# Reordering the prompt attention of a hybrid decoder step: transposes, fills, roots and the last heads

## The chip, the cores and the metric

The kernel runs on one core of one Trainium2 chip. The metric is the device time of one execution in microseconds (us); lower is better. Engines are named as the profile names them: PE is TensorE (matrix multiplies and transposes), ACT is ScalarE, DVE is VectorE, POOL is GpSimd, and SP is the queue that issues nearly all of the DMAs.

## What is computed

One layer of a decoder, for a prompt of 1024 tokens and for 8 samples of 4 new tokens each (32 rows, which the kernel treats as tile 8 behind the eight prompt tiles of 128 rows). Only the parts that the change touches are shown:

```python
u, v, cq, ckv, kpe = split_in(rms_norm(xp, g_mix[l]) @ w_in[l])
a_out, _ = chunk_gmlp(u, v, w_s[l], b_s[l], ln_v_g[l], ln_v_b[l])
ckv_n = rms_norm(ckv, g_kv_a[l])
q = mla_queries(cq, pos_p, g_q_a[l], w_uq[l], g_qk_q[l])      # 8 heads x 96, normalised and rotated
k, vv = mla_keys_values(ckv_n, kpe, pos_p, w_uk[l], w_uv[l], g_qk_k[l])
b_out = mla_prompt_attend(q, k, vv)                           # causal softmax over 1024 keys
xp = xp + merge_out(a_out, b_out, g_out_a[l], g_out_b[l], w_o[l])

def merge_out(a_out, b_out, g_out_a, g_out_b, w_o):
    return jnp.concatenate([rms_norm(a_out, g_out_a), rms_norm(b_out, g_out_b)], axis=-1) @ w_o
```

The same runs for the samples, whose attention reads 4096 cached tokens each; then follow a memory attention and a gated feed-forward block. All data are float32.

## The kernel before

**Matrix products.** `mm3` (line 179) makes a float32 product from three matmuls of a high and a low half (`h`, `l` at the end of names; `split`, line 187, cuts them: the high half on ScalarE, the low half on VectorE). Inside the prompt attention the low half of every split is put into a list, `self.lows`, and issued by the next `flush` (line 204).

**First stage** (`phase1`, line 288). The rows of x are projected to u, v and the latents. The root of each row's mean square stands in `rs_tok`, one column a tile of rows. `squares(c)` (line 342) squares three tiles on ScalarE and takes their root in about eleven small steps (`rsqrt_steps`, line 214) on VectorE, or for the later tiles on GpSimd. `squares(2)` does tiles 6, 7 and the 32-row tile 8 together. A planner orders this stage on all engines but SP.

**Prompt attention** (`phase2a`, line 646). From the line with `manual_schedule` on, PE, ACT, DVE and POOL run in the order in which the code emits the instructions; SP's order is left to the planner. A *unit* is one head and one half of the queries, (h, G) with G = 0 or 1, four query tiles each. `head_unit` (line 936) gives its parts: scores `a` (matmuls, and the evacuation with the row's maximum on VectorE), exponential `e` (ScalarE, line 969), transposes `T` of the probabilities (line 977, copied by ScalarE, line 979), products with the values `V` (line 992), `copy` and `out`. A unit with G = 0 takes three steps and one with G = 1 four, so the eight heads take 56 steps, counted by `t`. In each step the loop emits: the pending low halves, the transposes of the unit's probabilities, outputs that are due, the exponentials of the scores of the step before, the scores of the *next* unit (`jobs`), the low halves again, the value products of the step before, and then everything that is placed in `extra[t]`; last, one piece of each running generator in `steps`.

What is placed in `extra`, by hand: `preps[h]` (line 918), four pieces a head that transpose the keys and queries of one half, in the order k0, q0, k1, q1, and split them; the projections and norms of heads 4 to 7 (`late`, from `proj_group`, line 850, whose last pieces rotate the queries and finish the keys on GpSimd, lines 607 to 610 and 907); and the `weight_sums` (line 809), 26 pieces that load two weight blocks, make four sums on GpSimd (lines 822 to 825) and store them for the feed-forward block. They share two buffers, so each load waits for the store of two pieces before.

The generators are `sample_prep` (line 1014), started in step 31, which makes the samples' query operands and fills `cn`, `bd` and four blocks `bdq` on GpSimd; then `pages_ahead`; and at the end of the stage `mix` (through `mix_steps`, line 1575), which normalises, transposes and stores the attention's output rows for the merge.

**Sample attention** (`phase2b`, line 1118). Its loop over pairs of cached pages emits in the same manner; prompt tiles 4 to 7 go through `mix_steps` at fixed places of that loop.

Of the kernel before, what the change touches and what calls it, by code (L numbers as in the profile page):

```python
# [13 lines left out]
P = 128  # L14
# [140 lines left out]
class Net:  # L155
# [96 lines left out]
    def constants(self, pool):  # L252
        nc, I = self.nc, self.I
        self.cols = self.t(pool, [P, NCOL], F32, "cols")
        nc.sync.dma_start(self.cols, I["cols"])
        self.ident = self.t(pool, [P, P], F32, "ident")
        self.ones = self.t(pool, [P, P], F32, "ones")
        nc.gpsimd.memset(self.ones, 1.0)

        nc.scalar.activation(self.t(pool, [P, 1], F32, "gelu"), self.ones[:, :1], AF.Gelu_apprx_tanh)  # L260
        self.cn = self.t(pool, [P, 258], F32, "cn")
        self.kpe = self.t(pool, [P, 9, 32], F32, "kpe")
        self.rs_tok = self.t(pool, [P, 9], F32, "rs_tok")
        self.sq_tok = self.t(pool, [P, 9], F32, "sq_tok")
# [23 lines left out]
    def phase1(self):  # L288
# [53 lines left out]
        def squares(c):  # L342

            ss = self.t(pl, [P, 3], F32, "ss", 3)
            if c == 2:
                nc.vector.memset(ss, 1.0)
            for i in range(3):
                xt = xts[3 * c + i]
                nc.scalar.activation(xt, xt, AF.Square, accum_out=ss[: xt.shape[0], i : i + 1])
            for _ in self.rsqrt_steps(pl, self.rs_tok[:, 3 * c : 3 * c + 3], ss, 1.0 / 1024, nc.gpsimd if c else None):  # L350
                pass
# [18 lines left out]
        for c, (o, n) in enumerate(CH):  # L370
            for k in range(8):
                self.split(xh[:, k, o : o + n], xl[:, k, o : o + n], xrs[2 * c + k // 4][:, k % 4], self.col("g_mix", k))
            if c == 1:
                squares(0)
# [13 lines left out]
        squares(1)  # L388
# [42 lines left out]
        for hf in range(2):  # L431
# [8 lines left out]
            for i0, i1 in ((0, 3), (3, 6), (6, 8), (8, 9)):  # L440
                m, tn = i1 - i0, TILES[i0][1]
                if hf == 0 and i0 == 3:
                    squares(2)
# [202 lines left out]
    def phase2a(self):  # L646
# [28 lines left out]
        gs = [self.proj_group(p, pp, 0, *g, st[0], c, ("mm", 5)) for g in groups]  # L675
        (qk, v), (qk1, _), (qk2, _) = gs
        for f in qk + v + qk1[:9] + qk2[:3]:
            f()
        norm, norm_s = qk1[9:], qk2[3:]
# [10 lines left out]
        order = [(h, G) for h in range(6) for G in range(2)] + [(6, 0), (7, 0), (6, 1), (7, 1)]  # L690
        units = [self.head_unit(pm, pp, h, G, st[h // 4], c) for h, G in order]
        preps = [self.head_prep(pm, pp, h, st[h // 4], c) for h in range(8)]
        _, v1 = self.proj_group(p, pp, 0, *groups[1], st[0], c)
        late = [self.proj_group(p, pp, 1, *g, st[1], c) for g in groups]
# [40 lines left out]
        def mix(G, ring):  # L735
            n = self.t(p, [P, 4, 4, 96], F32, ring, 2).rearrange("p m h d -> p (m h d)")
            hl = n[:, 512:].rearrange("p (k n) -> p k n", k=4)
            yield from self.mix_steps(
                pm, pp, 1, 2 * G, 2 * G + 2, lambda i: b_all[:, i], lambda j: hl, lambda j: n[:, :512], ("tp", 4)
            )  # L740

        E = mybir.EngineType
        with tc.manual_schedule(engines={E.PE, E.Activation, E.DVE, E.Pool}):
# [17 lines left out]
            for n, u in enumerate(units):  # L761
                for k, banks in enumerate(u["steps"]):
# [32 lines left out]
            for f in V:  # L795
                f()
            for t in sorted(outs):
                for f in outs[t]:
                    f()
            while steps:  # L800
                steps = [x for x in steps if next(x, 0) is None]
        nc.sync.dma_start(self.b_dram, b_all[:, 4:])
# [211 lines left out]
    def sample_prep(self, pp):  # L1014
# [29 lines left out]
        nc.gpsimd.memset(self.cn, 0.0)  # L1044
# [73 lines left out]
    def phase2b(self):  # L1118
# [30 lines left out]
        for i, src in ((6, self.b_last), (4, b4)):  # L1149
            flat = place()  # L1150
            hl = flat[:, :1024].rearrange("p (k n) -> p k n", k=4)
            mix = self.mix_steps(
                pa, ppt, 1, i, i + 2, lambda e, src=src: src[:, e % 2], lambda j, hl=hl: hl,
                lambda j, flat=flat: flat[:, j * 512 : j * 512 + 512], ("m", 1),
            )
            for n in range(5):
                at(2 * n + (2 if i == 6 else 5), 0, lambda mix=mix: next(mix, 0))
# [417 lines left out]
    def mix_steps(self, p, pp, z, i0, i1, src, new, nt, tt):  # L1575
# [10 lines left out]
        yield  # L1586
# [4 lines left out]
        yield  # L1591
        for i, n in enumerate(ns):
# [9 lines left out]
            elif z:  # L1602
# [786 lines left out]
```

## Time and profile before

| | us |
|---|---|
| median of 3 runs | 1879.51 (1877.55 to 1879.68) |
| profiled execution | 1879.13 |
| its span, first to last instruction | 1877.4 |
| TensorE busy | 1820.9 (97%) |
| VectorE busy | 1351.9 (72%) |
| ScalarE busy | 927.3 (49%) |
| GpSimd busy | 700.4 (37%) |
| mean granted clock of TensorE | 0.987 of full speed |

The stages follow one another in time: the first stage to about 198 us, the prompt attention to about 434 us, the sample attention after it. A row of a timeline reads: start, length, engine, line of the kernel, operation, what is written and read, and in brackets the idle time of the engine before it with what ended that. Busy time on TensorE is modelled; at half clock the same matmul is busy for longer. The line numbers are those of the kernel before.

### The profile page before, as it was taken

The numbers are of one execution on the slowest core, as the hardware profiler recorded it, in microseconds if no ns is written. First come the engines' busy times: TensorE is split into PE (matmuls) and PEld (weight loads), VectorE is DVE, ScalarE is ACT, GpSimd is POOL, SyncE is SP. The second block draws the span as 40 slices with busy tenths as digits, with TensorE's granted clock in tenths as the row PEclk, the third lists the DMA queues.
The fourth block names the chain that finished last, engine by engine and source line by source line (L and its number), as shares of the span: only waits on it lengthen the run. The fifth ranks groups of instructions, "written<-read, shape, count | busy, mean of one in ns | idle before, by whom it ended". The sixth has DMA issues, their size and how long they took to land.

```text
span 1877.4 us, 39366 instructions
## 1 busy us (share of the span) xinstructions
PE 1820.9 (97%) x14222; PEld 1713.6 (91%) x14222; DVE 1351.9 (72%) x2800; ACT 927.3 (49%) x1965; POOL 700.4 (37%) x862
## 2 busy tenths in 40 slices
PE   9999899888999999999899999999999999999999
PEld 8899677668999999999799988999999999999999
DVE  7864756565877668776744676788888888878664
ACT  7335676565555565555533455633333333344442
POOL 2021246533444444453313110167776677500000
PEclk9999999899999999999999999999999999999999
DMA  8102054556776666664554345322223222495252
GB/s 314 46 17 71 23 184 142 163 173 174 227 207 181 184 183 186 176 181 121 187 166 135 130 151 155 128 72 76 85 75 97 69 70 79 109 354 165 79 153 75
DMA packets 153187, 261.18 MB, mean 139 GB/s; under 512 B 20897, under 2 KB 97538, under 8 KB 152994
## 3 DMA queue, kind: packets, MB, share of 16 engines
q1 hardware_dynamic: 152130, 257.63, 44.6%
q8 instruction: 112, 1.84, 0.4%
q10 hardware_dynamic: 864, 1.05, 0.2%
q14 instruction: 81, 0.66, 0.1%
HBM read 212.79 MB, written 45.82 MB: 138 GB/s over the span
## 4 chain that ended last, share of the span: by engine, by line
PE 78%; issue 6%; DVE 4%; DMA 4%; SPq 3%; POOL 2%; ACT 2%; POOLq 0%; DVEq 0%; ACTq 0%
PE s L185 13%; PE d L185 12%; PE mm L185 9%; PE b L185 8%; PE F L185 7%; PE X L185 7%; PE E L185 7%; PE A L185 3%; PE y L185 3%; PE o L992 2%; DMA cT<-cT 2%; PE tp L977 1%; SPq L1297 1%; SPq L1301 1%; PE tp L185 1%
## 5 line engine op out<-in xcount | busy, mean ns | idle before, releaser
L185 PE MATMUL s<-w2h,ch 128*128 128x288 f32 (+1 forms) x1024 | 305.1, 298 | 0.0
L185 PE MATMUL s<-w2h,cl 128*128 128x288 f32 (+1 forms) x1024 | 297.4, 290 | 4.2 <-POOL cl L1329 4.2
L185 PE MATMUL s<-w2l,ch 128*128 128x288 f32 (+1 forms) x1024 | 296.0, 289 | 0.0
L185 PEld LDWEIGHTS s<-w2h,ch 128*128 128x128 f32 x1024 | 194.0, 189 | 8.3 <-issue 2.5
L185 PEld LDWEIGHTS s<-w2h,cl 128*128 128x128 f32 x1024 | 193.8, 189 | 6.3 <-POOL cl L1329 6.3
L185 PEld LDWEIGHTS s<-w2l,ch 128*128 128x128 f32 x1024 | 194.3, 190 | 0.0
L1372 DVE TENSOR_REDUCE ss<-sq 128x16 f32<-128x1024 f32 x128 | 155.3, 1214 | 32.1 <-ACT sq L1369 31.6
L1329 POOL TENSOR_TENSOR cl<-cT,ch 128x512 fp32r<-128x512 f32 x64 | 82.8, 1294 | 124.9 <-ACT ch L1325 116.1
L1369 ACT ACTIVATE sq<-s 128x512 f32<-128x512 f32 x128 | 76.6, 598 | 89.7 <-PE s L185 89.7
L1366 ACT ACTIVATE sq<-s 128x512 f32<-128x512 f32 x128 | 76.8, 600 | 72.9 <-PE s L185 72.4
L191 ACT CAST a<-brb 128x528 fp32r<-128x528 f32 x77 | 48.8, 634 | 112.8 <-PE d L185 108.7
L185 PE MATMUL d<-a,w 128*128 128x264 f32 x768 | 95.4, 284 | 1.0 <-DVE G L2166 1.0
L185 PEld LDWEIGHTS d<-a,w 128*128 128x128 f32 x768 | 94.3, 188 | 1.2 <-issue 1.2
L192 DVE TENSOR_TENSOR a<-brb,a 128x528 fp32r<-128x528 f32 x77 | 54.4, 707 | 56.3 <-ACT a L191 56.3
L2037 POOL TENSOR_TENSOR lo<-s,hi 128x1024 fp32r<-128x1024 f32 x20 | 62.8, 3141 | 45.7 <-ACT hi L2036 45.7
L185 PE MATMUL mm<-whi,xh 128*128 128x256 f32 (+3 forms) x272 | 77.9, 288 | 0.0
L185 PE MATMUL mm<-wlo,xh 128*128 128x256 f32 (+3 forms) x272 | 77.5, 287 | 0.0
L185 PE MATMUL mm<-whi,xl 128*128 128x256 f32 (+3 forms) x272 | 77.4, 288 | 0.0
L2092 ACT COPY a<-A 128x264 f32<-128x264 f32 x43 | 16.1, 375 | 118.7 <-PE A L185 113.9
L1325 ACT CAST ch<-cT 128x512 fp32r<-128x512 f32 x128 | 73.4, 626 | 2.6 <-PE tp L1005 1.6
L185 PE MATMUL d<-a,hi 128*128 128x264 f32 x552 | 72.0, 284 | 0.0
L2155 POOL TENSOR_TENSOR cv<-cv,row 128x1056 f32<-128x1056 f32 x22 | 63.5, 2887 | 19.1 <-ACT cv L2154 19.1
(743 smaller groups left out, 6381.8 us busy)
## 6 DMA issues: line engine op xcount, KB each, us to landing
cT<-cT SPq DMA_DIRECT2D x256, 160.0 KB, 2.9
ck<-ck SPq DMA_DIRECT2D x256, 144.0 KB, 3.4
raw<-w_up SPq DMA_DIRECT2D x44, 512.0 KB, 3.6
wsumd<-wsum SPq DMA_DIRECT2D x26, 512.0 KB, 3.4
actd<-cv SPq DMA_DIRECT2D x44, 264.0 KB, 2.4
brb<-actd SPq DMA_DIRECT2D x44, 264.0 KB, 5.6
wsum<-w_down SPq DMA_DIRECT2D x22, 512.0 KB, 3.6
raw<-wsumd SPq DMA_DIRECT2D x20, 512.0 KB, 3.7
```

The lines of the kernel that those rows point to most:

```text
L185: self.nc.tensor.matmul(out, l, r, start=first and i == 0, stop=last and i == len(seq) - 1)
L191: {"act": nc.scalar.copy, "pool": nc.gpsimd.tensor_copy, "dve": nc.vector.tensor_copy}[eng](hi, src)
L192: low = lambda: nc.vector.tensor_tensor(lo, src, hi, ALU.subtract)
L977: nc.tensor.transpose(tp[:, z * P : z * P + P], u[e][:, j * P : j * P + P], self.ident)
L992: nc.tensor.matmul(u["o"][g : g + 64, o : o + m * P], s["v"][:, j, h % 4], th[:, z * P : (z + m) * P], start=j == 0, stop=b == len(banks) - 1,
L1325: nc.scalar.copy(d["h"][:, k], src[k])
L1329: (nc.vector if k else nc.gpsimd).tensor_tensor(d["l"][:, k], src[k], d["h"][:, k], ALU.subtract)
L1366: nc.scalar.activation(sq[:, 0], ps[:, :, n0 : n0 + 256], AF.Square)
L1369: nc.scalar.activation(sq[:, 1], pt.rearrange("p (e d) -> p e d", e=2), AF.Square)
L1372: yield lambda: nc.vector.tensor_reduce(s["ss"][:, g0 : g0 + 2].rearrange("p e (z h) -> p z e h", z=2), sq.rearrange("p z e (h d) -> p z e ...
L2037: eng.tensor_tensor(lo, src, hi, ALU.subtract)
L2155: nc.gpsimd.tensor_tensor(cv, cv, row, ALU.mult)
```

## The change

- *Roots.* `squares` takes a range of tiles and an engine. Tiles 6 and 7 are done together on GpSimd, tile 8 alone on VectorE. `rs_tok` is set to 1 once.
- *Sample tile's projection.* Queries and keys of heads 0 to 3 for tile 8 are projected within steps 0 to 6 and no longer ahead of the attention.
- *Transposes ahead.* The pieces of `preps` move so that scores follow their query tile by two steps or more (before, mostly one), and the first half's keys by three.
- *Last heads.* The order of units becomes (5,0), (6,0), (5,1), (7,0), (6,1), (7,1) where it was (5,0), (5,1), (6,0), (7,0), (6,1), (7,1).
- *Late projections and sums.* The second group of `late` moves one step ahead. 18 of the weight sums are placed in steps 4 to 28, none in 29 to 35, and 8 in steps 36 to 47; before, the 26 were spread evenly over steps 4 to 47.
- *Fills.* `sample_prep` emits the fills of `bdq` and `cn` first, and the copy into `qr` and the fill of `bd` one step later; all that follows comes one step later.
- *Merge.* `mix` runs over four tiles as one generator with finer pieces, in the prompt attention (tiles 0 to 3) and in the sample attention (tiles 4 to 7).

```diff
+        nc.vector.memset(self.rs_tok, 1.0)
...
-        def squares(c):
-            ss = self.t(pl, [P, 3], F32, "ss", 3)
-            if c == 2:
-                nc.vector.memset(ss, 1.0)
-            for i in range(3):
-                xt = xts[3 * c + i]
-                nc.scalar.activation(xt, xt, AF.Square, accum_out=ss[: xt.shape[0], i : i + 1])
-            for _ in self.rsqrt_steps(pl, self.rs_tok[:, 3 * c : 3 * c + 3], ss, 1.0 / 1024, nc.gpsimd if c else None):
+        def squares(i0, i1, e=None):
+            n, w = i1 - i0, TILES[i0][1]
+            ss = self.t(pl, [P, 3], F32, "ss", 4)[:w, :n]
+            for i in range(i0, i1):
+                nc.scalar.activation(xts[i], xts[i], AF.Square, accum_out=ss[:, i - i0 : i - i0 + 1])
+            for _ in self.rsqrt_steps(pl, self.rs_tok[:w, i0:i1], ss, 1.0 / 1024, e):
                 pass
...
-                    squares(2)
+                    squares(6, 8, nc.gpsimd)
+                    squares(8, 9)
...
-        gs = [self.proj_group(p, pp, 0, *g, st[0], c, ("mm", 5)) for g in groups]
-        (qk, v), (qk1, _), (qk2, _) = gs
-        for f in qk + v + qk1[:9] + qk2[:3]:
+        (qk, v), (qk1, _) = (self.proj_group(p, pp, 0, *g, st[0], c, ("mm", 5)) for g in groups[:2])
+        for f in qk + v + qk1[:9]:
             f()
-        norm, norm_s = qk1[9:], qk2[3:]
+        norm = qk1[9:]
...
-        order = [(h, G) for h in range(6) for G in range(2)] + [(6, 0), (7, 0), (6, 1), (7, 1)]
+        order = [(h, G) for h in range(5) for G in range(2)] + [(5, 0), (6, 0), (5, 1), (7, 0), (6, 1), (7, 1)]
...
+        tok_s, _ = self.proj_group(p, pp, 0, *groups[2], st[0], c)
...
-        spread(norm_s, 0, 4)
+        spread(tok_s, 0, 7)
         for h in range(1, 8):
             b = 7 * (h - 1)
-            put(preps[h], {3: (9, 10, 11, 13), 4: (22, 23, 25, 26), 6: (36, 37, 39, 40), 7: (40, 41, 44, 46)}.get(h, (b + 1, b + 2, b + 2, b + 4)))
+            put(preps[h], {3: (9, 10, 12, 13), 5: (28, 29, 34, 35), 6: (32, 33, 41, 42), 7: (39, 38, 44, 46)}.get(h, (b, b + 1, b + 3, b + 4)))
         spread(late[0][0], 11, 21)
-        spread(late[1][0], 15, 25)
+        spread(late[1][0], 14, 24)
         spread(late[0][1], 22, 27)
-        spread(late[1][1], 26, 31)
+        spread(late[1][1], 25, 30)
...
-            extra[4 + j * 45 // len(sums)].append(lambda x=x: self.weight_sums(half(), *x))
+            extra[4 + j * 26 // 18 if j < 18 else 36 + (j - 18) * 13 // 8].append(lambda x=x: self.weight_sums(half(), *x))
...
-        def mix(G, ring):
...
+        def mix():
+            n = [self.t(p, [P, 4, 4, 96], F32, r, 2).rearrange("p m h d -> p (m h d)") for r in "kq"]
+            hl = [x[:, 512:].rearrange("p (k n) -> p k n", k=4) for x in n]
+            for k, _ in enumerate(self.mix_steps(
+                pm, pp, 1, 0, 4, lambda i: b_all[:, i], lambda j: hl[j], lambda j: n[j // 2][:, :512], ("tp", 4)
+            )):
+                if k not in (0, 2):
+                    yield
...
-                            outs[t + 3].append(lambda: steps.extend((mix(0, "k"), mix(1, "q"))))
+                            outs[t + 3].append(lambda: steps.append(mix()))
...
-            for f in V:
-                f()
-            for t in sorted(outs):
-                for f in outs[t]:
+            for fs in [V] + [outs[t] for t in sorted(outs)] + [[]] * 4:
+                for f in fs:
                     f()
-            while steps:
                 steps = [x for x in steps if next(x, 0) is None]
...
-        nc.gpsimd.tensor_copy(qr, qs[:, :, 64:].unsqueeze(2).broadcast_to([NS, 8, 4, 32]))
-        nc.gpsimd.memset(self.bd, 0.0)
         bds = []
         for pr in range(4):
             bds.append(self.t(p, [P, 2, NS], F32, "bdq", 4))
             nc.gpsimd.memset(bds[pr], 0.0)
+        nc.gpsimd.memset(self.cn, 0.0)
+        yield
+        nc.gpsimd.tensor_copy(qr, qs[:, :, 64:].unsqueeze(2).broadcast_to([NS, 8, 4, 32]))
+        nc.gpsimd.memset(self.bd, 0.0)
         yield
...
             nc.tensor.transpose(tp[:, k * P : k * P + P], self.cns[:, k], self.ident)
-        nc.gpsimd.memset(self.cn, 0.0)
...
@@ mix_steps @@
             nc.scalar.activation(nt(i - i0)[:tn], n, AF.Square, accum_out=r[:, i - i0 : i - i0 + 1])
-        yield
+            if z:
+                yield
         self.rsqrt(p, r, r, 1.0 / 512)
         yield
         for i, n in enumerate(ns):
             nc.scalar.activation(n, n, AF.Copy, scale=r[:, i : i + 1])
-        yield
+            if z and i % 2:
+                yield
```

More of the change, by code (lines that the diff above doesn't have):

```diff
@@ L373, in phase1 @@
             if c == 1:
-                squares(0)
+                squares(0, 3)
         def proj(w, i, n, tag=("mm", 5)):
@@ L387, in phase1 @@
         tload(6)
-        squares(1)
+        squares(3, 6, nc.gpsimd)
         for i in range(7, 9):
@@ L733, in sample @@
             yield from self.pages_ahead()
-        def mix(G, ring):
[L736 to L740, printed above, removed]
+        def mix():
[6 more added lines that the diff above has]
+                    yield
         E = mybir.EngineType
@@ L794, in phase2a @@
             self.lows = None
-            for f in V:
-                f()
-            for t in sorted(outs):
-                for f in outs[t]:
+            for fs in [V] + [outs[t] for t in sorted(outs)] + [[]] * 4:
+                for f in fs:
                     f()
-            while steps:
                 steps = [x for x in steps if next(x, 0) is None]
+            assert not steps
         nc.sync.dma_start(self.b_dram, b_all[:, 4:])
@@ L1148, in phase2b @@
         nc.sync.dma_start(b4, self.b_dram)
[L1149 to L1157, printed above, removed]
+        flat = [place() for _ in range(2)]
+        hl = [x[:, :1024].rearrange("p (k n) -> p k n", k=4) for x in flat]
+        mix = self.mix_steps(
+            pa, ppt, 1, 4, 8, lambda i: (b4, self.b_last)[i // 6][:, i % 2], lambda j: hl[j],
+            lambda j: flat[j // 2][:, j % 2 * 512 : j % 2 * 512 + 512], ("m", 1),
+        )
+        for n in range(11):
+            at(n + 3 if n < 7 else 2 * n - 3, 0, lambda: next(mix, 0))
         def mixed_load(k):
@@ L1601, in mix_steps @@
                 nc.sync.dma_start(self.mix_dram[:, z * 4 : z * 4 + 4, o : o + w], hl[:, :, :w])
-            elif z:
+            if z and i < m - 1:
                 yield
```

## The prediction

> **What bounds the kernel now.** I read the page's totals first, then the busy time by stretch, then TensorE's waits, then the timelines around the longest of them.
>
> ```profile
> span 1877.4 us, 39366 instructions
> PE 1820.9 (97%) x14222; PEld 1713.6 (91%) x14222; DVE 1351.9 (72%) x2800; ACT 927.3 (49%) x1965; POOL 700.4 (37%) x862
> ```
>
> TensorE is the bound of the whole, so only its gaps and its slow stretches can be won: 1877.4 - 1820.9 = 56.5 us of gaps. The stretch that the change rewrites is the prompt attention:
>
> ```profile
> 198.00:434.00 236.00, 209.82 (x1360) 156.09 (x1359) 144.27 (x496) 152.48 (x434) 102.72 (x156) 0.93 0.44 140
> 40.00:60.00 20.00, 20.00 (x172) 19.70 (x170) 18.59 (x66) 10.48 (x25) 8.95 (x14) 1.00 0.25 88
> 66.00:69.00 3.00, 3.00 (x16) 3.00 (x16) 2.44 (x14) 0.00 (x0) 0.00 (x0) 0.50 0.74 233
> 232.00:236.00 4.00, 3.66 (x20) 3.17 (x19) 2.97 (x12) 2.53 (x7) 0.00 (x0) 0.64 0.07 5
> 328.00:332.00 4.00, 4.00 (x18) 2.38 (x17) 2.18 (x12) 0.00 (x0) 0.00 (x0) 0.59 0.41 131
> 356.00:363.00 7.00, 6.85 (x26) 5.05 (x26) 2.68 (x10) 4.14 (x13) 5.19 (x8) 0.51 0.47 152
> 390.00:393.00 3.00, 3.00 (x11) 1.54 (x9) 1.92 (x8) 1.65 (x5) 0.13 (x1) 0.53 0.97 308
> 420.50:424.50 4.00, 4.00 (x23) 2.83 (x23) 1.45 (x8) 3.84 (x7) 0.00 (x0) 0.57 0.00 0
> ```
>
> The columns after the stretch are its length and the busy time of TensorE, weight loads, VectorE, ScalarE, GpSimd, then the granted clock. In 198 to 434 us nearly half of all the gaps lie (236.00 - 209.82 = 26.2 us), at a mean clock of 0.93. The six short rows are the slow stretches that the change could touch: TensorE looks full but works at about half speed, so each loses its length times one minus the clock: 3.00 x 0.50 = 1.5 us, then 1.4, 1.6, 3.4, 1.4 and 1.7.
>
> ```profile
> PE s L185 <- DVE qTl L198: 5.4, 5, 2.0
> PE tp L977 <- ACT cn L1045: 5.4, 1, 5.4
> PE tp L977 <- ACT pr L969: 5.1, 4, 2.4
> ```
>
> These are the largest waits of that stage: scores that wait for the low half of transposed queries (five times), one wait for a fill of GpSimd, and probability transposes that wait for an exponential. In the timeline of TensorE (start, length, idle before it) they, and the gate's wait of the stage before, are:
>
> ```profile
> 64.78 1.20 PE L185 MATMUL mm<-vgh,wsh 128*128 128x512 f32 x4 [3.57 <-ACT vgh L191]
> ...
> 231.59 0.33 PE L185 MATMUL s<-kTh,qTh 96*128 96x128 f32 x1 [0.64 <-ACT qTh L195]
> ...
> 232.37 0.33 PE L185 MATMUL s<-kTh,qTl 96*128 96x128 f32 x1 [0.34 <-DVE qTl L198]
> ...
> 312.30 0.33 PE L185 MATMUL s<-kTh,qTl 96*128 96x128 f32 x1 [1.13 <-DVE qTl L198]
> ...
> 326.45 0.41 PE L185 MATMUL s<-kTh,qTl 96*128 96x320 f32 x1 [1.98 <-DVE qTl L198]
> ...
> 356.15 0.69 PE L977 MATMUL tp<-ident,pr 128*128 128x128 f32 x2 [5.37 <-ACT cn L1045]
> ...
> 388.35 0.33 PE L185 MATMUL s<-kTh,qTl 96*128 96x128 f32 x1 [1.66 <-DVE qTl L198]
> ...
> 420.30 0.80 PE L977 MATMUL tp<-ident,pr 128*128 128x128 f32 x5 [2.45 <-ACT pr L969]
> ```
>
> Each slow stretch starts some 4 us after the beginning of such a gap. The attention's steps can be dated: a row with 128 columns is the first score of a head, 231.59 that of head 1 (step 3), 388.35 that of head 7 (step 42), so a step takes (388.35 - 231.59) / 39 = 4.0 us.
>
> **The change part by part.** No matrix work is added or dropped; all of it is order.
>
> *Roots of the token rows (first stage).* The gate's last tiles need the root of rows 6 to 8. Before, one root serves all three, after tile 8's square; it runs on GpSimd behind the causal select:
>
> ```profile
> 35.30 0.19 ACT L349 ACTIVATION_READ_ACCUMULATOR a_all<-a_all 128x1 f32 x1
> ...
> 50.88 0.20 POOL L245 TENSOR_TENSOR rs_tok<-rqh,rqy 128x3 f32<-128x3 f32 x1
> 51.12 0.48 ACT L458 ACTIVATE gv<-st,rs_tok 128x256 f32<-128x256 f32 x1 [3.14 <-POOL rs_tok L245]
> ```
>
> The squares of tiles 6 and 7 are there at 35.5; their root now needs nothing else and can be done by about 42. But VectorE is busy 18.59 of 20 us there, so the chain can't shrink by those 9 us: only work for later use steps back behind it. I keep 1.5 us of the 3.57 and let the slow stretch go: 2.0 + 1.5 = 3.5 us won (bounds: 5.1 won, 1 lost, as the order of this stage is a planner's). Tile 8's own root goes to VectorE: about eleven operations on 32x1, off the path, since tile 8 comes last.
>
> *The sample tile's projection out of the start.* Tile 8's queries and keys are projected in steps 0 and 1 rather than ahead of the attention. Its ScalarE work stood in front of the first key split:
>
> ```profile
> 201.54 0.47 ACT L874 COPY qs<-mm 32x384 f32<-32x384 f32 x1 [0.41 <-PE mm L185]
> 201.92 0.48 ACT L880 ACTIVATE hsq<-mm 32x384 f32<-32x384 f32 x1
> ...
> 204.50 0.20 ACT L878 ACTIVATE hsq<-mm 32x64 f32<-32x64 f32 x1
> ...
> 205.19 0.18 ACT L878 ACTIVATION_READ_ACCUMULATOR hsq<-mm 32x1 f32 x1
> ```
>
> That is 0.4 + 0.8 + 0.8 = 2.0 us sooner. Its twelve matmuls come back in steps 0 and 1:
>
> ```profile
> 200.30 0.33 PE L185 MATMUL mm<-wqh,cqh 128*32 128x384 f32 x1
> ...
> 201.17 0.34 PE L185 MATMUL mm<-wqh,cql 128*32 128x384 f32 x1
> ```
>
> Six in 1.04 us, so at most 2.1 us for twelve, up to 4.2 at half clock: I take 2.3. Net 0.3 lost. Head 1's queries are now transposed two steps ahead, and the waits of 0.64 and 0.34 go, the slow stretch at 232 with them (1.4). What is late next is the transpose that waits for the fourth exponential in step 3, under a microsecond. Together 0.98 + 1.4 - 0.3 = 2.1 us (bounds 4 won, 1 lost).
>
> *Heads 2 to 7.* Every query tile but the two of step 0 is now cut at least two steps ahead: the gaps of 1.13, 1.98 and 1.66 go, with two slow stretches (1.6, 1.4): 7.8 us. VectorE's copies ran late there because roots of tile 8 and the sample scores were queued between the split and the scores; now the split stands a step before them.
>
> *What this presses on.* Head 4's keys need GpSimd's part of the normalised keys, and GpSimd also makes the weight sums in program order. Eleven sums rather than nine now stand ahead of the first group's part, thirteen rather than eleven ahead of the second.
>
> ```profile
> 261.30 0.73 POOL L822 TENSOR_TENSOR wsum<-wsum 128x256 f32<-128x256 f32 x1 [3.89 <-DMA wsum<-w_down]
> ...
> 281.69 0.74 POOL L822 TENSOR_TENSOR wsum<-wsum 128x256 f32<-128x256 f32 x1 [1.89 <-DMA wsum<-w_down]
> ...
> 291.87 1.05 POOL L907 TENSOR_TENSOR k<-kr,hr 128x512 f32<-128x512 f32 x1 [2.13 <-DVE hr L236]
> ...
> 309.37 1.05 POOL L907 TENSOR_TENSOR k<-kr,hr 128x512 f32<-128x512 f32 x1 [4.46 <-DVE hr L236]
> ...
> 305.50 0.64 PE L930 MATMUL tp<-ident,k 128*96 128x128 f32 x4
> ```
>
> A sum comes every (281.69 - 261.30) / 4 = 5.1 us, paced by its load. So the first part, done at 292.9 before, is done at 292.9 + 2 x 5.1 - 2.1 = 301.0. TensorE transposes these keys at 305.5 in step 22; in step 21 it is there at 301.5: no wait, but no margin. The second part followed after 12.0 us of other work and 1.05 of its own: 314.0, against 301.5 + 3 x 4.0 = 313.5, less the 1.1 us won on the way. A new wait of 2 us (0 to 4, the upper end with a slow stretch); behind it on TensorE's queue stands everything from step 25 on, and ScalarE and VectorE wait with it. Heads 2 to 7 come to 5.8 us.
>
> *The fills.* The wait of 5.37 us is ScalarE's copy into `cn`, behind GpSimd's fill of it, behind a weight sum whose load was late:
>
> ```profile
> 350.12 0.72 POOL L822 TENSOR_TENSOR wsum<-wsum 128x256 f32<-128x256 f32 x1 [6.15 <-DMA wsum<-w_down]
> ...
> 355.39 0.30 POOL L1044 MEMSET cn<- 128x258 f32 x1
> ```
>
> With the change no sum stands in steps 29 to 35, the fills of `cn` and the blocks come a step before their use, and the big copies follow them. The last sum ahead has its load behind it while GpSimd waits for the sample root. Gap and slow stretch go: 5.37 + 3.4 = 8.8 us. The sample chain ends one step later, which nobody waits for before the next stage.
>
> *The last steps.* All four squares of the merge stood on ScalarE ahead of the last exponential:
>
> ```profile
> L1585 ACT ACTIVATE k<-b_all 128x512 f32<-128x512 f32 x2 | 1.2, 624 | 0.0
> ...
> L1585 ACT ACTIVATION_READ_ACCUMULATOR k<-b_all 128x1 f32 x2 | 0.4, 190 | 0.0
> ```
>
> Four times 0.81 is 3.2 us; two now come after it: 1.6 of the 2.45 us, and with a gap under 1 us the slow stretch (1.7): 3.3 us. The remaining transposes move behind the last head, where they fill waits. The last merge store now stands ahead of the store that the next stage reads back, under 1 us on SP's queue, either way.
>
> Sum: 3.5 + 2.1 + 5.8 + 8.8 + 3.3 = 23.5 us, less 2 us for five places where something 0.4 us later takes over: **21.5 us**. The profiled execution took 1879.13 us (span 1877.4 and 1.7 around it), 0.4 below the median of the three runs (1879.51), so 1857.6 us.
>
> **On the slow stretches.** The row of 390 to 393 us shows a clock of 0.53 after a gap of 1.66 us. [...]
>
> **The rivals.**
> (a) *Half of the waits come back elsewhere.* For it: ScalarE and VectorE are busy 152 and 144 of 236 us, and at each place another operation is close behind. Against it: the longest waits are single late queue entries. Only the fills in full and about 2 us more: 11 us, 1868.
> (b) *Slow stretches stay.* The one at 232 us followed waits none of which reached 1 us, so what is left could still bring it on. The four after gaps under 3 us (1.4 + 1.6 + 1.4 + 1.7 = 6.1) stay: 1863.7. [...]
> (c) *The fills aren't first in practice:* SP's order is the planner's, and a late load still precedes them. Without those 8.8 us: 1866.4.
> (d) *Slower:* the weight sums hold up head 4. If the packed sums took c us each, the first part would be done at 261.3 + 6c + 9.1 (the last sum 3.1, from 281.69 to 284.8; the rotation of the queries 4.9, to 289.7 where the wait of 2.13 begins; its own 1.05). At c = 9.0 that is 324.4, a wait of 22.9 us and 3.4 us of half clock: 4.8 us more than is won, 1883.9. It decides from about c = 8.8, against 5.1 measured.
>
> **How the numbers follow.** Forecast 0.58, (a) 0.17, (b) 0.08, (c) 0.07, (d) 0.06, no change 0.04. A measurement of this kernel can tell about 0.2%, 3.8 us. Range: with the better bounds (5.1, 4, 7.8, 8.8, 3.3, and nothing that takes over) 29.0 us are won, 1850; with the worse ones in the first stage, at the start and at head 4, 21.5 - 4.5 - 3.1 - 2 = 11.9, 1867; (a) reaches 1868. So 1850 to 1869. Faster 0.90, same 0.04, slower 0.06.
>
> **What would show it.** Right: no wait of TensorE on `cn`; those on `qTl` under 1 us in sum; the clock at 1.00 where the rows above show half; a busy share above 0.93 of the attention's span, that span near 217 us. Wrong: a wait for `k` of GpSimd over 4 us near head 4, a first stage that is longer, or the attention's span within 5 us of 236.

## The result and the profile after

| | before | after |
|---|---|---|
| median of 5 runs | 1879.51 us (1873.68 to 1881.17) | 1869.24 us (1869.04 to 1872.15) |
| ratio after to before | | 0.9956 (95% interval 0.9938 to 0.9973) |
| span of the profiled execution | 1877.4 us | 1867.5 us |

The change won about 10 us where 21.5 were forecast; 1869.24 us lies just above the range (1850 to 1869). The page of the kernel after begins:

```profile
span 1867.5 us, 39356 instructions
PE 1819.1 (97%) x14222; PEld 1713.6 (92%) x14222; DVE 1349.1 (72%) x2789; ACT 927.7 (50%) x1965; POOL 703.9 (38%) x862
```

Gaps of TensorE fell from 56.5 to 1867.5 - 1819.1 = 48.4 us. The busy time by stretch (length, TensorE, weight loads, VectorE, ScalarE, GpSimd, granted clock), the attention first:

```profile
198.00:424.00 226.00, 207.38 (x1371) 156.15 (x1369) 145.15 (x488) 154.21 (x438) 105.09 (x159) 0.95 0.45 145
60.00:80.00 20.00, 16.23 (x105) 14.81 (x103) 14.73 (x42) 5.44 (x11) 0.00 (x0) 0.83 0.17 55
200.00:240.00 40.00, 33.58 (x181) 26.54 (x181) 25.72 (x92) 25.18 (x80) 5.77 (x14) 0.83 0.11 31
300.00:320.00 20.00, 14.34 (x94) 10.84 (x93) 13.67 (x41) 8.95 (x18) 18.98 (x29) 0.91 0.50 159
320.00:340.00 20.00, 18.85 (x125) 14.39 (x124) 11.09 (x39) 11.32 (x34) 10.94 (x15) 0.91 0.59 191
340.00:360.00 20.00, 19.44 (x147) 14.25 (x147) 12.51 (x42) 15.77 (x37) 14.13 (x25) 1.00 0.58 192
```

The attention takes 226 us, not 217, at a busy share of 207.38 / 226 = 0.92. The long wait near 356 us is gone. The new hole is at 300 to 340 us, and in it GpSimd is busy for 18.98 of 20 us. TensorE's waits within the attention (total, times, longest):

```profile
PE tp L930 <- POOL k L907: 5.6, 2, 2.9
PE tp L977 <- ACT pr L969: 5.2, 6, 1.3
PE s L185 <- DVE pr L964: 2.3, 6, 1.2
...
PE s L185 <- DVE qTl L198: 0.6, 2, 0.3
```

As forecast, the waits on `qTl` fell from 5.4 to 0.6 us and the one on `cn` is not in the list. At the top now stands GpSimd's part of head 4's keys. Those waits in TensorE's timeline, with the gate's wait of the first stage and a wait at the start of the sample attention:

```profile
64.82 2.07 PE L185 MATMUL mm<-vgh,wsh 128*128 128x512 f32 x4 [3.77 <-ACT vgh L191]
...
306.19 0.89 PE L930 MATMUL tp<-ident,k 128*96 128x128 f32 x4 [2.77 <-POOL k L907]
...
319.28 0.64 PE L930 MATMUL tp<-ident,k 128*96 128x128 f32 x4 [2.87 <-POOL k L907]
...
437.69 0.77 PE L1344 MATMUL s<-bd,krq 128*128 128x128 f32 x2 [4.20 <-ACT S L1347]
```

**An account by marks.** Five points of TensorE's timeline cut each run: Q, the first projection of queries (181.79 us here); the first scores of heads 2 (255.63) and 5 (346.96); the first page score (422.62); and the end. The projection of the sample tile lies between Q and head 2 in both kernels.

| us | before | after | won | forecast |
|---|---|---|---|---|
| up to Q | 180.2 | 181.8 | -1.6 | 3.5 (roots) |
| Q to head 2 | 74.2 | 73.8 | 0.4 | 2.1 (start) |
| head 2 to head 5 | 87.8 | 91.3 | -3.5 | 2.7 (1.13 + 1.98 + 1.6 - 2) |
| head 5 to first page score | 90.9 | 75.7 | 15.2 | 15.2 (8.8 + 3.1 + 3.3) |
| rest | 1444.4 | 1444.9 | -0.5 | 0 |

The late half came out as forecast, to a tenth, which is partly luck, since its parts are off by up to 1.6 us both ways (below); the early half lost instead of winning. Two of the prediction's signs of being wrong came: more than 4 us of waits for GpSimd's `k` near head 4 (5.6 in sum), and a longer first stage.

### The profile page after: what moved, and what is told of

The parts are those of the page before. It is cut to its first block, busy times and chain, and to the rows that moved or that the text cites. A ratio compares the mean times of both kernels' runs of the same rounds, so it can differ in the third digit from the quotient of the medians.

```text
span 1867.5 us, 39356 instructions
## 1 busy us (share of the span) xinstructions
PE 1819.1 (97%) x14222; PEld 1713.6 (92%) x14222; DVE 1349.1 (72%) x2789; ACT 927.7 (50%) x1965; POOL 703.9 (38%) x862
## 4 chain that ended last, share of the span: by engine, by line
PE 79%; issue 6%; DVE 5%; DMA 3%; SPq 3%; POOL 2%; ACT 2%; DVEq 0%; POOLq 0%; ACTq 0%
PE s L185 14%; PE d L185 12%; PE mm L185 9%; PE b L185 8%; PE X L185 7%; PE E L185 7%; PE F L185 7%; PE A L185 3%; PE y L185 2%; PE o L992 2%; PE tp L977 1%; PE tp L185 1%; SPq L1297 1%; PE o L1444 1%; DMA ck<-ck 1%
## 5 line engine op out<-in xcount | busy, mean ns | idle before, releaser
L1366 ACT ACTIVATE sq<-s 128x512 f32<-128x512 f32 x128 | 76.8, 600 | 74.7 <-PE s L185 74.3
L1368 DVE TENSOR_TENSOR S<-s,S 128x64 f32<-128x64 f32 x128 | 28.0, 219 | 57.6 <-ACT sq L1366 57.3
```

The lines of the kernel that those rows point to most:

```text
L1366: nc.scalar.activation(sq[:, 0], ps[:, :, n0 : n0 + 256], AF.Square)
L1368: nc.vector.tensor_tensor(S, ps[:, :, sc : sc + 32], S, ALU.add)
```

## The experiments

The theory after the result: the fills and the last heads did what was forecast; the gain was lost in front of them, to GpSimd's weight sums ahead of head 4's keys, to the order of the first stage, and at the start. The rivals: ScalarE and VectorE are close behind everywhere, so that any wait removed comes back; or the slow stretches of the clock only moved. Each result below gives the median and the ratio to the kernel before on the same chip. The runs come from several chips, on which the median of the kernel before lies between 1875.5 and 1879.5 us, so small differences between numbers go by the ratios.

**1. The old roots.**

```diff
-                    squares(6, 8, nc.gpsimd)
-                    squares(8, 9)
+                    squares(2)        # one root for tiles 6, 7, 8
```

> The kernel after, but one root for tiles 6, 7 and 8 again, as before. Theory (the new order of the first stage costs time, since the causal select and the weight cast now stand behind the earlier root): the first stage ends at 198.7 us instead of 200.3, so 1.6 us less than after, about 1867.6. Rival (the roots are worth what the prediction said): the stage is 3.5 us longer than after's, 1872.7. Second rival (the 1.6 us is only another order of a planner that the roots don't cause): the stage stays at 200.3 and the time at 1869.2.

1867.16 us, 0.9946 (0.9928 to 0.9965). Q stands at 181.2 (the end of the stage, which the expectation names, moves with it: both came 1.64 us later after than before), the gate's wait is 3.57 (3.77 with the new roots). The forecast's 3.5 us are refuted; that the new roots cost 1.6 is not shown either, since the kernel before has Q at 180.2 with the same first stage. Over all profiles without the split of number 7, Q is at 180.2, 181.2, 181.3 and 180.3 with the old roots (mean 180.8) and at 181.8, 182.4, 180.8, 181.4, 180.9, 181.0 and 181.2 with the new (mean 181.4): 0.6 us later, less than either group scatters.

**2. The sums moved.**

```diff
-extra[4 + j * 26 // 18 if j < 18 else 36 + (j - 18) * 13 // 8]
+extra[4 + j * 45 // 26 if j < 15 else 36 + (j - 15) * 15 // 11]
```

> The kernel after, but with the weight sums placed at before's spacing up to step 28 (15 sums, nine instead of eleven ahead of the first late rotation) and the other 11 in steps 36 to 50. Theory (GpSimd's sums make head 4's keys late): the two waits of 2.77 and 2.87 us for GpSimd's part of the keys are under 1 us, and the two stretches with a clock of 0.91 over 20 us (1.8 us each) are at 1.00: 5.6 + 3.6 = 9 us less than after, about 1860. Rival (ScalarE and VectorE are close behind everywhere, so another wait takes over): the waits go but waits for pr and qTl grow, under 3 us less than after, 1866 to 1869.

1859.88 us, 0.9911 (0.9893 to 0.9929): the largest step from the kernel after, some 8 us. (The last 11 sums stand in steps 36 to 49.) GpSimd's timeline in the kernel after, where the eleventh sum, the rotations (L607 to L610) and the keys follow without a gap:

```profile
296.96 1.68 POOL L823 TENSOR_TENSOR wsum<-wsum 128x256 f32<-128x256 f32 x1
...
299.53 0.73 POOL L825 TENSOR_TENSOR wsum<-wsum 128x256 f32<-128x256 f32 x1
300.23 0.72 POOL L607 TENSOR_TENSOR rp<-q,tq_c 128x256 f32<-128x256 f32 x1
...
305.09 1.04 POOL L907 TENSOR_TENSOR k<-kr,hr 128x512 f32<-128x512 f32 x1
```

and with the sums moved, with the row of TensorE's timeline that used to wait:

```profile
286.78 0.73 POOL L825 TENSOR_TENSOR wsum<-wsum 128x256 f32<-128x256 f32 x1
287.47 0.72 POOL L607 TENSOR_TENSOR rp<-q,tq_c 128x256 f32<-128x256 f32 x1
...
295.13 1.05 POOL L907 TENSOR_TENSOR k<-kr,hr 128x512 f32<-128x512 f32 x1 [2.77 <-DVE hr L236]
...
303.34 0.64 PE L930 MATMUL tp<-ident,k 128*96 128x128 f32 x4
```

The keys come 10 us sooner, 7 us ahead of TensorE. Waits for `pr` did grow (those behind VectorE from 2.3 to 4.1 us), as the rival says, but by far less than was won. Of the two stretches that the theory puts at a clock of 1.00, that of 320 to 340 us is there; 300 to 320 us still runs at 0.83.

**3. The sample tile back ahead of the attention.**

```diff
-        for f in qk + v + qk1[:9]:
+        for f in qk + v + qk1[:9] + qk2[:3]:
...
-        spread(tok_s, 0, 7)
+        spread(norm_s, 0, 4)
```

> The kernel after, but with the sample tile's queries and keys projected ahead of the attention, as before. Theory (the move loses at the start and, by the rotation of the sample queries that stands ahead of the first weight sum on GpSimd, delays all sums by 3.2 us): the first sum comes at 238.6 instead of 241.7, the two waits for head 4's keys fall from 5.6 to about 1 us, the start loses no more than it won: 3 to 6 us less than after, 1863 to 1866. Rival (the prediction's step: the move is worth 2.1 us): head 1's first score comes 2 us later, total 1869 to 1871.

1864.13 us, 0.9932 (0.9917 to 0.9948). Half of the theory fell: the first sum did come earlier (239.06 for 241.73 us), and head 4's keys by 3 us, but TensorE came earlier too, so the waits grew from 5.6 to 7.5 us:

```profile
303.14 0.64 PE L930 MATMUL tp<-ident,k 128*96 128x128 f32 x4 [3.05 <-POOL k L907]
...
316.22 1.09 PE L930 MATMUL tp<-ident,k 128*96 128x128 f32 x4 [4.45 <-POOL k L907]
```

Q to head 2 took 71.5 us, the shortest of all; number 5 shows that this was not the tile.

**4. The kernel before with the fills alone** (with the sums of number 2, so that none stands in steps 29 to 35).

```diff
+        nc.gpsimd.memset(self.cn, 0.0)
+        yield
         nc.gpsimd.tensor_copy(qr, ...)
         nc.gpsimd.memset(self.bd, 0.0)
...
-        nc.gpsimd.memset(self.cn, 0.0)
```

> The kernel before with one part of the change: the samples' fills first, and no weight sum in steps 29 to 35 (15 sums ahead at before's spacing, 11 in steps 36 to 50). Theory (the fills' wait and its slow stretch were real and nothing was behind them): no wait for cn, step of head 6 8.8 us earlier, 8.8 us less than before, about 1870.7. Rival (half of it comes back in the steps behind, where VectorE's low halves are late): 3 to 5 us less, 1875.

1868.02 us, 0.9950 (0.9934 to 0.9966). Head 5 to the first page score falls from 90.9 to 80.5 us, 10.4 for the 8.8 forecast. With the sums placed as in number 2, this part alone wins as much as the whole change does.

**5. Sums and sample tile together.** The edits of numbers 2 and 3.

> The kernel after with both: 15 sums at before's spacing and 11 from step 36, and the sample tile projected ahead of the attention. Theory (two separate losses: sums ahead of head 4's keys, and the tile's projections in the ring of transposes at the start): from the first projection of queries to head 2's first score 71.5 us, as with the tile alone (73.8 in the kernel after), no wait for GpSimd's keys, another 2.2 us less than with the sums alone, about 1857.7. Rival (both changes mend the same wait): as with the sums alone, 1859.9.

1861.77 us, 0.9926 (0.9907 to 0.9946). Q to head 2 is 74.7 us, not 71.5: the theory of a separate loss by the tile is refuted. With the new transposes and the tile ahead, four runs show 71.5, 74.7, 73.3 and 75.2 (numbers 3, 5, 8 and 11); with the tile in steps 0 to 6, 73.2 to 75.1. Most of the difference between numbers 3 and 5 is the clock, with TensorE, ScalarE and VectorE in the same order up to there:

```profile
220.00:240.00 20.00, 18.33 (x84) 13.61 (x84) 13.55 (x53) 11.59 (x25) 1.65 (x5) 0.68 0.14 44
```

Number 3 has 0.92 in that stretch, and 0.82 in the 20 us before it, where number 5 has 0.89.

**6. The squares of the first pages later.** With the sums of number 2.

```diff
-at(n + (6 if 0 <= Q < 2 else 3), 0, self.quad_sums, ...)
+at(n + (6 if -1 <= Q < 2 else 3), 0, self.quad_sums, ...)
```

> The kernel after with 15 and 11 sums, and in the sample attention the squares of the first page quad three steps later on ScalarE. Theory (the 4.1 us wait of the first page scores comes from ScalarE, which waits for the page's load with the copy of S behind it): that wait is gone and the clock of the next 20 us is at 0.95 or above: 4 to 6 us less than with the sums alone, 1854 to 1856. Rival (the pages themselves are late and the first product of probabilities waits for them instead): 0 to 1 us less, 1859 to 1860.

1861.02 us, 0.9929 (0.9908 to 0.9951). The wait for the copy of `S` is gone, and one for the pages' rotated keys has taken its place:

```profile
PE s L1344 <- POOL krq L1316: 2.7, 1, 2.7
```

From the first page score to the end it is 1441.3 us, with the sums alone 1441.4: nothing is won, as the rival says. What waits is another operation than it names, the scores and not a product of probabilities. GpSimd's waits for the pages' loads ahead of that rotation (`krq`, L1314) come to 27.5 us in the whole run, nine waits with 6.6 us as the longest; that the pages are late at this one of the nine is the author's reading, no row shows it.

**7. The split of u's second half behind the gate's.** ScalarE's timeline of the kernel after shows what stood ahead of the gate's tiles 6 and 7: the last gelu (an activation function) of u (L487), which waits for TensorE, and then a weight split of 2.2 us:

```profile
61.10 0.47 ACT L487 ACTIVATE a_all<-mm,rs_tok 32x256 f32<-32x256 f32 x1 [1.97 <-PE mm L185]
61.47 2.19 ACT L191 CAST whi<-wraw 128x1152 fp32r<-128x1152 f32 x2
63.56 0.41 ACT L463 ACTIVATE gsq<-gv 32x256 f32<-32x256 f32 x1
63.88 0.89 ACT L191 CAST vgh<-gv 128x256 fp32r<-128x256 f32 x2
```

```diff
+                if name == "u1":      # after the split of vgh, vgl of tile 7: order alone
+                    for x, y in zip(xs, gate_last[0]):
+                        tc.add_manual_dep(x.ins, y.ins.name, ...)
```

> The kernel after, but in the first stage the split of the second half of u's weights (2.2 us on ScalarE, 2.7 us on VectorE) is put behind the split of the gate's tiles 6 and 7 by an order of instructions alone. Theory (the roots of tiles 6 and 7 are early enough, and the gate waits only for this split, which the planner puts ahead): the gate's wait falls from 3.77 to under 2 us, the slow stretch behind it is shorter or gone, and the stage ends 2 to 4 us earlier: 1865 to 1867. Rival (ScalarE's last gelu of u and VectorE's chain are as late themselves): wait over 3 us, 1869.

1867.45 us, 0.9953 (0.9938 to 0.9968). The gate's wait falls to 2.81 us, not under 2, and Q to 180.1: less than the theory says, more than the rival.

**8. The kernel before with fills, transposes ahead, late groups and last heads**; roots, sample tile and merge as before, sums as in number 2.

```diff
-order = [(h, G) for h in range(6) ...] + [(6, 0), (7, 0), (6, 1), (7, 1)]
+order = [(h, G) for h in range(5) ...] + [(5, 0), (6, 0), (5, 1), (7, 0), (6, 1), (7, 1)]
...                                     # and the places of preps and late as in the change
```

> The kernel before with the fills, 15 and 11 sums (the run of the fills alone), and the transposes ahead, the late groups' step and the last heads' order; the roots, the sample tile and the merge are those of before. Theory (the prediction's term of 7.8 us for heads 2 to 7 was right as long as GpSimd's keys are not late): waits for qTl under 1 us, no wait for GpSimd's keys, 7 to 10 us less than with the fills alone (1868.0): 1858 to 1861. Rival (the gaps come back as waits for pr): 3 us less, 1865.

1859.28 us, 0.9913 (0.9896 to 0.9931): 7 to 9 us under the fills alone, without a wait for GpSimd's keys, and with 0.3 us of waits for `qTl`. The time is the theory's. Where it was won is not shown: in the profiles, 7.0 us apart, 1.5 lie between heads 2 and 5, 1.6 from head 5 to the first page score and 0.8 from Q to head 2, but 1.0 up to Q and 2.1 behind the first page score, where the two kernels have the same code.

**9. Three buffers for the sums**, which stay in their places.

```diff
-half = lambda: self.t(pm, [P, 2, 2, 256], F32, "wsum", 2)
+half = lambda: self.t(pm, [P, 2, 2, 256], F32, "wsum", 3)
...
-th = u["t", b] = self.t(p, [P, 512], F32, "pth", 6)
+th = u["t", b] = self.t(p, [P, 512], F32, "pth", 5)
```

> The kernel after with three buffers for the weight sums instead of two (and five instead of six for the copied probabilities, to make room); the same 18 sums stand in steps 4 to 28. Theory (a sum every 5.1 us because each load waits for the store of two sums before): the sums keep up with the steps, GpSimd's keys for head 4 are ready before TensorE asks, both waits under 1 us, 5 to 9 us less than after, 1860 to 1864. Rival (GpSimd's own work is what is full: 3.1 us a sum and the rotations between): still a sum every 4 to 5 us, waits of 1 to 2 us each, 1866 to 1868.

1861.11 us, 0.9922 (0.9902 to 0.9942). As many sums stand ahead as in the kernel after, but the keys are in time:

```profile
295.26 1.05 POOL L907 TENSOR_TENSOR k<-kr,hr 128x512 f32<-128x512 f32 x1 [1.60 <-DVE hr L236]
...
303.47 0.64 PE L930 MATMUL tp<-ident,k 128*96 128x128 f32 x4
```

The first keys are done 9.8 us sooner. So the sums are held up by the two buffers, a load waiting for the store of two sums before, and not by GpSimd's own work. The pace over the first eleven falls from 5.4 to 4.5 us, still above the 3.1 us of GpSimd's work, and it goes on waiting for loads (18.7 us in eleven waits in the whole run): that was enough here, with nothing to spare shown.

**10. The split moved, with the old roots.** The edits of numbers 7 and 1.

> The kernel after with the split of u's second half behind the gate's, and one root for tiles 6, 7 and 8 as before. Theory (the prediction's root was real but hidden by that split): with the split away the gate waits for the late root, 3.5 us and more where the new roots left 2.81, and the stage is 0.7 to 2 us longer than with the new roots. Rival (the root is not on this path at all): 2.6 to 2.9 us, the same stage.

1864.55 us, 0.9944 (0.9924 to 0.9964). Neither theory nor rival foresaw this: the wait is the smallest of all, the clock stays full, and Q is at 176.7 us.

```profile
62.70 1.20 PE L185 MATMUL mm<-vgh,wsh 128*128 128x512 f32 x4 [1.46 <-ACT vgh L191]
```

```profile
60.00:80.00 20.00, 18.54 (x147) 17.43 (x146) 17.43 (x59) 7.02 (x14) 0.00 (x0) 1.00 0.17 55
```

ScalarE's timelines show a first difference. This run, then number 7 with the new roots:

```profile
42.73 1.05 ACT L191 CAST wsh<-ws 128x1024 fp32r<-128x1024 f32 x1 [0.96 <-POOL ws L415]
```

```profile
46.41 1.05 ACT L191 CAST wsh<-ws 128x1024 fp32r<-128x1024 f32 x1 [4.53 <-POOL ws L414]
```

With the new roots GpSimd does the root of tiles 6 and 7 ahead of the causal select (`ws`), and the gate's weights come 3.7 us later. But VectorE, which waits for them, has made that up by the time it takes the low halves of the three tiles before (57.88 us there, 57.67 here). What differs behind them is its order: with the new roots, steps of tile 8 stand ahead of the last steps of tiles 6 and 7, and one of them waits for ScalarE. VectorE's rows, this run, then number 7:

```profile
61.44 0.74 DVE L482 TENSOR_TENSOR gv<-gv,rows 128x256 f32<-128x256 f32 x2
62.11 0.40 DVE L473 TENSOR_REDUCE rv<-gsq 32x4 f32<-32x256 f32 x1
```

```profile
62.38 0.41 DVE L473 TENSOR_REDUCE rv<-gsq 32x4 f32<-32x256 f32 x1 [0.69 <-ACT gsq L472]
...
63.05 0.40 DVE L482 TENSOR_TENSOR gv<-gv,rows 128x256 f32<-128x256 f32 x1
```

So tiles 6 and 7 are split at 63.49 for 61.96 us. Number 11, also with the new roots, has the same order and the same wait of 0.69 us; numbers 12 and 13, with the old ones, have neither. The planner makes this order, and no run changes it alone.

**11. Three corrections together**: the edits of numbers 2, 3 and 7.

> The kernel after with three corrections together: 15 and 11 sums, the sample tile projected ahead of the attention, and the split of u's second half behind the gate's. Theory (separate losses that add up): no wait for GpSimd's keys, a gate's wait of 2.8 us, 10 us less than after, 1857 to 1860. Rival (the slow stretches of the clock fall elsewhere and take half of it): 1862 to 1864.

1861.54 us, 0.9921 (0.9901 to 0.9941): the keys are in time (head 2 to head 5 in 85.3 us), Q is at 178.2, but nothing is gained on number 2. The rival's time, at least.

**12. Sums, old roots and the split moved.** The edits of numbers 1, 2 and 7.

> The kernel after with 15 and 11 sums, one root for tiles 6, 7 and 8, and the split of u's second half behind the gate's. Theory (the first stage loses 5 us in the kernel after, the sums 8 to 9, and both can be had at once): gate's wait 1.5 us, first projection of queries at 176.7 instead of 181.8, no wait for GpSimd's keys, 1855 to 1858. Rival (what is won at one place is lost as slow clock at another, as in the three corrections together): 1860 to 1863.

1859.38 us, 0.9915 (0.9898 to 0.9933). The gate waits 2.25 us, Q is at 177.2 and head 2 to head 5 takes 84.0 us, so both corrections work where they stand; the total is still that of number 2 alone. In this profile the rest, from the first page score on, takes 1446.2 us where number 2 has 1441.4; its code is the same but for the planner's order. The kernels with the split moved have 1442.9 to 1447.7 there, the others 1440.9 to 1445.4, and it stays open whether that is the split or chance.

**13. The same, with the squares of number 6.**

> The same with the squares of the first page quad three steps later in the sample attention. Theory (the wait of 4 to 5.7 us for the copy of S is partly the squares, partly the pages): 2.7 us of wait for the pages' rotated keys remain, 1 to 2 us less than without this edit. Rival (all of it is the pages): the same within 1 us.

1858.93 us, 0.9916 (0.9902 to 0.9930): no difference that can be told, the rival again. The gate waits 1.46 us, where number 12, with the same code in the first stage, has 2.25.

**14. The kernel after, unchanged.**

> The kernel after, unchanged. Theory (slow stretches of the clock come or stay away by chance at the same gaps): the waits are those of the first profile within 0.2 us (3.77 for the gate, 2.8 and 2.9 for GpSimd's keys), but the clock of 60 to 80, 200 to 240 and 300 to 340 us and the times between the heads differ by 1 to 3 us. Rival (the slow stretches follow from the waits): the same clocks, the same times within 0.3 us.

1868.47 us, 0.9958 (0.9944 to 0.9972). The same stretches as above:

```profile
60.00:80.00 20.00, 16.24 (x115) 14.78 (x114) 15.53 (x47) 5.84 (x11) 0.00 (x0) 0.91 0.17 55
200.00:240.00 40.00, 32.71 (x175) 24.91 (x174) 25.42 (x91) 24.20 (x76) 5.16 (x11) 0.83 0.11 32
300.00:320.00 20.00, 14.57 (x96) 10.40 (x96) 14.80 (x43) 9.25 (x20) 18.98 (x28) 0.96 0.50 159
320.00:340.00 20.00, 18.51 (x117) 14.26 (x117) 10.95 (x36) 9.92 (x32) 10.28 (x15) 0.87 0.55 182
```

```profile
305.50 0.64 PE L930 MATMUL tp<-ident,k 128*96 128x128 f32 x4 [1.54 <-POOL k L907]
...
318.64 1.09 PE L930 MATMUL tp<-ident,k 128*96 128x128 f32 x4 [2.97 <-POOL k L907]
```

The gate's wait is the same to 0.01 us (3.76), while its stretch runs at 0.91 rather than 0.83. So the clock differs at the same gap, as the theory says. One of the two waits for the keys differs by 1.2 us, against it; a likely reading is that the wait is what is left between two queues, and so takes up what the clock did before it. The times between marks differ by 0.6 us up to Q, 1.2 to head 2 and 0.5 to head 5, rather less than the 1 to 3 expected. A term of 1 or 2 us can't be told from one profile.

## Why the prediction was wrong

**The step that failed most is "What this presses on".** The mechanism was named, with its rows: thirteen and eleven sums ahead, a sum every 5.1 us, keys with no margin. Its size was wrong: a wait of 2 us, 4 with a slow stretch at most. Head 2 to head 5 took 91.3, 91.8, 90.2, 92.1, 90.5 and 91.9 us in the six runs that start from the kernel after and leave the sums where it puts them (mean 91.3), and 86.9, 83.1, 84.1, 85.0, 85.3, 84.0 and 84.0 in the seven with the sums moved or three buffers (mean 84.6): the place of the sums costs 6.7 us. The first keys were forecast for 301.0 and came at 306.1. Three things made them later. The first sum began 3.2 us later (241.73 for 238.57). Its load (SPq is the DMA queue) and the rows of GpSimd ahead of it, in the kernel before and then after:

```profile
234.31 2.68 SPq L819 DMA_DIRECT2D wsum<-w_up  x4
...
238.57 0.72 POOL L822 TENSOR_TENSOR wsum<-wsum 128x256 f32<-128x256 f32 x1 [8.02 <-DMA wsum<-w_up]
```

```profile
237.39 2.68 SPq L819 DMA_DIRECT2D wsum<-w_up  x4
...
240.23 0.45 POOL L607 TENSOR_TENSOR rp<-qs,tq_c 32x128 f32<-32x128 f32 x1 [26.96 <-DVE rn L903]
...
241.73 0.72 POOL L822 TENSOR_TENSOR wsum<-wsum 128x256 f32<-128x256 f32 x1
```

The rotation of the sample queries, which the change moved into steps 0 to 6, now ends just ahead of the first sum; but the load, too, is issued 3.1 us later, behind VectorE's split of the weights that hold its buffer (`wvl`, from 236.94 us), and at the 4.3 us from issue to sum of before it would have landed at 241.7. The prediction counted neither; with the tile ahead again (number 3) the load is back at 234.31 and the sum at 239.06. Second, the pace of 5.1 was that of four sums; over the first eleven it was (296.14 - 241.73) / 10 = 5.4, which made the eleventh 1.1 us later still than two sums at 5.1 behind the ninth of before. Third, one operation took 1.68 instead of 0.73 us. Two more differences from the forecast nearly cancel: the 2.1 us taken off for the start did not come, and the 2.13 us that the keys waited for VectorE before fell away.

Two waits, not one, came of it, 5.6 us in this profile and 1.8 to 7.5 in the six runs. In number 1 they are only 1.8 us and the stretch still takes 90.2: there TensorE waits 1.5 us for `pr` between heads 4 and 5 and the clock is 0.94, some 1.8 us, where number 2 has no such wait and a clock of 1.00. How the 6.7 us divide between the waits and what follows them is therefore not shown.

**Roots** (3.5 won forecast, none seen; the mean of 0.6 lost is within the scatter). The root of tiles 6 and 7 was not what the gate waited for. The prediction saw the root end 0.04 us before the gelu that uses it and took it for the cause of the wait that ends 14 us later; between them stood the split of u's weights (numbers 7 and 10). Once that is away the old roots are the better ones, Q at 176.7 to 177.2 (numbers 10, 12 and 13) for 178.2 and 180.1 (11 and 7), with the order that the planner then gives VectorE. Nor was the new root done by 42 us: it ended at 44.3, as one step of it took GpSimd 4.30 us (39.45 to 43.75), where the same step took 0.68 in the kernel before (46.26). VectorE was busy for all of the 4.30 us, but also for all of the 0.68 us; what held the step up is not shown.

**The start** (2.1 forecast): Q to head 2 took 74.2 and 74.1 us with the code of before, and a mean of 73.9 in the ten runs with that of the kernel after, 0.3 won. The waits of 0.64 and 0.34 us are gone, but the transpose behind them now waits 1.31 us for `pr`, where under a microsecond was expected, and the next one 0.79. Those two waits were not what sets the clock there: 200 to 240 us ran at 0.83 after and 0.87 before.

**Heads 2 to 7, without the wait** (4.7 forecast up to head 5): 87.8 - 84.6 = 3.2 us won, and the `qTl` waits went as written.

**Fills, heads 5 to 7 and merge** (8.8 + 3.1 + 3.3): 10.4, then 80.5 - 78.9 = 1.6, then 3.2 to the 75.7 us of the kernel after: the sum is exact by luck, as its parts are off by +1.6, -1.5 and -0.1 us. That a gap under 1 us brings no slow stretch, on which 1.7 us of the merge's term rest, was the author's estimate, and no run tried it alone: in the kernel before, 232 to 236 us ran at 0.64 after waits of 0.79, 0.64 and 0.34 us; in the kernel after, TensorE's longest wait from 410 to 426 us is one of 1.1 us, and 325 to 424 us ran at 1.00.

Of the rivals, (a) gave nearly the right time (1868) for another reason: the waits did not come back everywhere, new ones came at one place and one stage did not win. (d) is the right mechanism at the pace of before: it needs no sum of 8.8 us to cost 7. (b) is partly right: the stretch near 234 us stayed (234 to 238 us at 0.60 after), while the four behind 325 us are gone (325 to 424 us at 1.00). (c) is refuted by number 4. The forecast with the sums moved (number 2, 1859.88) is 2.3 us from the 1857.6 predicted, though partly for other reasons, as the first stage still wins nothing there. One reading of the prediction is off as well: not each slow stretch starts some 4 us after its gap begins. In the long gap that starts at 350.78 us the granted clock is 0.81 over 352 to 353 us and 0.50 over 353 to 354 us.

## What to carry to other kernels

When a change moves work off the path on an engine that runs in the order of the code, follow the last item of that queue up to the moment when the bound engine asks for it, with every instruction that now stands ahead of it, and write the margin beside the error of the pace: here a margin of zero was entered as a wait of 2 us. Spread work that is paced by its buffers where nobody waits behind it, or give it one buffer more: here that took the ratio from 0.9956 to 0.9911 and 0.9922 (numbers 2 and 9). And a late producer next to a wait is not its cause until the queue between them has been read line by line.

## What the runs showed of the hardware

At the gate one wait was varied, and it was TensorE's only gap from 60 to 80 us: busy time and wait fill the 20 us, 16.43 and 3.57 in the kernel before, 18.54 and 1.46 in number 10. The granted clock over 60 to 80 us was 1.00 with a wait of 1.46 us (two profiles), 1.00 with 2.25, 0.91 and 1.00 with 2.81, and 0.83 or 0.91 in all eleven profiles with 3.57 to 3.77 us. So one gap of 2.81 us had a slow stretch behind it and another of that length had none. In the attention of the kernel before a still shorter gap had one: the clock was 0.53 over 390 to 393 us after the gap of 1.66 us, with no other wait of TensorE from 380 to 390 us (busy for 8.35 of 10 us). So the length of a gap alone does not decide here; what else does was not tried.

What half a clock means for one matmul, in the kernel before: those of `whi` and `xl` (128x256) are busy for 0.41 us each over 66 to 69 us, at 0.50, and for 0.28 us over 72 to 74 us, at 1.00.

At the same gap the kernel after lost, by the clock alone, 20 x 0.09 = 1.8 us in one profile and 20 x 0.17 = 3.4 in another. By this estimate the clock is one reason why two profiles of one kernel differ, here by 0.5 to 1.2 us between marks.
